# Alternating two token tiles between two PSUM banks in five column blocks of one feed-forward stage

## The chip, the cores and the metric

The program runs on one core of a Trainium2 chip. The metric is device microseconds (us) of one execution; the time before is the median of three runs. The engines that matter here are TensorE (PE in the profile), which does matrix products and transposes, ScalarE (ACT) and VectorE (DVE), which convert and combine data, and SyncE (SP), which issues the weight loads. Each engine works through its own instructions in order.

## The reference

The reference is a two-layer decoder trunk on 256 tokens of width 1024: a first layer with a gated linear recurrence, a second with dilated attention, and a SwiGLU feed-forward block before and after each mixer, so four feed-forward stages in all. Each has this form, with an inner width of 2816:

```python
def swiglu(x, w_in, w_out):
    gate, up = jnp.split(x @ w_in, 2, axis=-1)
    return (jax.nn.silu(gate) * up) @ w_out
...
x = layer_norm(DEEPNORM_ALPHA * x + 0.5 * swiglu(x, ffn_w_in[layer, 1], ffn_w_out[layer, 1]),
               ln_g[layer, 2], ln_b[layer, 2])
```

## The kernel before

All matrices are float32, and every product of two of them is made as three products of parts: each operand is split into a high part (`_hi`, rounded to the matrix unit's short form) and the rest (`_lo`), and `mm3` (line 93 and on) adds hi·hi, hi·lo and lo·hi into one PSUM bank. Line 91 is the one place that issues a product, line 101 the one that issues a transpose.

Weights arrive as half pieces of 128 x 1024 floats (512 KB). `half_piece` loads one into `raw` (six buffers), ScalarE casts it to `w_hi` (line 130; line 107 for weights that are sums), VectorE subtracts to `w_lo` (line 131; line 108), with nine buffers for each. Loads, casts and subtractions are issued ahead of their use in the order of a list (`feed`), and a scheduler then places them among the other instructions of ScalarE and VectorE.

A feed-forward stage (`ffn`) runs over 11 column blocks j = 0 to 10; a block is 256 columns of the gate and the same 256 of the up projection, side by side in one PSUM bank of 512 columns for each of the two token tiles (128 tokens, t = 0 and 1). An ordinary block does four things:

- 24 products for each tile (8 steps k over the width of 1024, three products each) into one bank (`natural`);
- the gate: `sg` = SiLU of the first 256 columns on ScalarE (line 478), `gated` = `sg` times the other 256 on VectorE (line 481);
- `rest`, put off until a later `flush`: four transposes of `gated` on TensorE (`mm<-ident,gated`) and their split into `h_hi` on ScalarE and `h_lo` on VectorE (lines 107 and 108);
- the output products of the block two before it (`prj.part(t, j - 2, w)`), 12 for each tile, which read `h_hi` and `h_lo` of that block and add into the long-lived banks `yy`.

`flush` runs inside the block, after the products of the first tile and before the gate of that tile, and again after the second. What it finds in the list is the `rest` of an earlier block.

The stage that is changed is the second, `ffn(2, ...)`, from about 308 us to about 500 us of the span. In it blocks 3 with 4 and 7 with 8 go through `two_blocks`, a seven-product scheme over two blocks. That function finishes block j + 1 before block j: it flushes the `rest` of block 4 (of block 8) itself, and leaves that of block 3 (of block 7) in the list. Ordinary blocks under the diff are therefore 2, 5, 6, 9 and 10. After block 10 there is no output part; the tail of `finish` begins with the products of block 8 and then block 9 for the first half of the columns, 6 products each.

PSUM tiles named `mm` come from a pool of four banks in the order in which they are asked for; those named `yy` have their own two pairs.

Of the kernel before, what the change touches and what calls it, by code (L numbers as in the profile page):

```python
# [16 lines left out]
NT = SEQ // P  # L17
DM = 1024
KD = DM // P
# [19 lines left out]
PAIRS = {0: (4, 8), 1: (3, 7), 3: (3, 7)}  # L39
# [10 lines left out]
def trunk_kernel(  # L50
# [33 lines left out]
    def bank():  # L84
        return psum.tile([P, 512], F32, name="mm", bufs=4)
# [4 lines left out]
    def mm(ps, lhsT, rhs, start, stop, **kw):  # L90
        tc.keep_in_program_order(nc.tensor.matmul(ps, lhsT=lhsT, rhs=rhs, start=start, stop=stop, **kw))  # L91

    def mm3(ps, a, b, first, last, **kw):

        (ahi, alo), (bhi, blo) = a, b
        mm(ps, ahi, bhi, first, False, **kw)
        mm(ps, ahi, blo, False, False, **kw)
        mm(ps, alo, bhi, False, last, **kw)

    def turn(ps, src):  # L100
        tc.keep_in_program_order(nc.tensor.transpose(ps, src, ident))  # L101
# [4 lines left out]
    def split(hi, lo, src):  # L106
        nc.scalar.copy(hi, src)  # L107
        nc.vector.tensor_tensor(lo, src, f32(hi), ALU.subtract)  # L108

    def duo(tag, bufs, pool=act, shape=(2, SEQ)):  # L110
        hi = pool.tile([P, *shape], F32R, name=f"{tag}_hi", bufs=bufs)
        lo = pool.tile([P, *shape], F32R, name=f"{tag}_lo", bufs=bufs)
        return hi, lo

    def at(pair, *idx):
        return pair[0][(slice(None),) + idx], pair[1][(slice(None),) + idx]
# [35 lines left out]
    def take(n=2):  # L152

        pump(n - len(ready))
        w, ready[:n] = ready[:n], []
        return w
# [15 lines left out]
    def cols(w, start, n):  # L172
        h, c = divmod(start, HALF)
        return at(w[h], slice(c, c + n))

    def tok(t):
        return slice(t * P, (t + 1) * P)

    def halves(ps):
        return ps.rearrange("p (m s) -> p m s", m=2)  # L180

    xT = [act.tile([P, KD, SEQ], F32R, name=f"xT{i}") for i in range(2)]
# [20 lines left out]
    def late_loads():  # L203
        for dst_, src in ((xn[0], x[tok(0), :]), (xn[1], x[tok(1), :]), (par, rg_par), (dst, dist), (qsc, q_scale)):
            tc.keep_in_program_order(nc.sync.dma_start(dst_, src))

    def softplus_prep():
        lam = par[:, 7 * KR:8 * KR]
        tmp = work.tile([P, 5, KR], F32, name="spt", tag="hh")
        t = [tmp[:, i, :] for i in range(5)]  # L210
        nc.scalar.activation(t[0], lam, AF.Abs)
        nc.scalar.activation(t[0], t[0], AF.Exp, scale=-1.0)
        nc.vector.tensor_scalar_add(t[1], t[0], 2.0)
        nc.vector.reciprocal(t[1], t[1])
        nc.vector.tensor_mul(t[1], t[0], t[1])
        nc.vector.tensor_mul(t[2], t[1], t[1])
        nc.vector.tensor_scalar_mul(t[3], t[2], 1.0 / 19.0)
        for d in (17.0, 15.0, 13.0, 11.0, 9.0, 7.0, 5.0, 3.0):
            nc.vector.scalar_tensor_tensor(t[3], t[3], 1.0 / d, t[2], ALU.add, ALU.mult)
        nc.vector.scalar_tensor_tensor(t[3], t[3], 1.0, t[1], ALU.add, ALU.mult)  # L220
        nc.vector.tensor_scalar(t[4], lam, -1.0, 0.0, ALU.mult, ALU.max)
        nc.vector.scalar_tensor_tensor(t[4], t[3], 2.0, t[4], ALU.mult, ALU.add)
        for i, f in enumerate((4.0, -8.0)):
            nc.vector.tensor_scalar_mul(sp[i], t[4], f)

    def load_ln(i, tag="o", bufs=4):
        gb = [[act.tile([P, 512], F32, name="gb", tag=f"{tag}_{('hi', 'lo')[j]}", bufs=bufs) for j in range(2)]
              for _ in range(2)]
        for r in range(2):
            for h in range(2):  # L230
                tc.keep_in_program_order(
                    nc.sync.dma_start(gb[r][h], ln[i, r, h * 512:(h + 1) * 512].partition_broadcast(P)))
        return gb
# [82 lines left out]
    def natural(ps, t, w, ks=range(KD)):  # L316

        for k in ks:
            mm3(ps, at(xT, k, tok(t)), cols(w[k // 4], (k % 4) * 512, 512), k == 0, k == KD - 1)

    def channel_half(ps, w, m):
        for k in range(KD):
            mm3(ps, cols(w, k * 256 + m * P, P), at(xT, k), k == 0, k == KD - 1)
# [75 lines left out]
        for i in range(NJ - TAIL, NJ):  # L399
            order(w_out[idx, i])  # L400

    def ffn(ln_i, turn_x, ahead, pairs=()):
        hs, gated = {}, {}
        later = []
        sums = {}
# [32 lines left out]
        def two_blocks(j):  # L438

            xs = [act_.rearrange("p k s -> p (k s)") for act_ in sums["tmp"]]  # L440
            flat = lambda n: xs[n]
            part = lambda q, t: (lambda k: at(xT, 4 * q + k, tok(t)))
            named = lambda n: (lambda k: at(sums[n], k))
            a, b, c = (bank() for _ in range(3))
            product(a, part(0, 0), True, False)
            nc.scalar.copy(flat(0), a)
            product(c, named("s1"), True, False)
            nc.scalar.copy(flat(1), c)
            flush()
            product(b, named("s2"), True, False)  # L450
            nc.vector.tensor_tensor(flat(2), b, flat(0), ALU.add)
            product(c, named("s4"), False)
            nc.vector.tensor_tensor(flat(3), c, flat(2), ALU.add)
            gate(flat(3), 0, j + 1)
            w = take()
            for t in range(NT):
                prj.part(t, j - 2, w)
            product(b, named("s3"), False, False)
            nc.vector.tensor_tensor(flat(2), b, flat(0), ALU.add)
            nc.vector.tensor_tensor(flat(1), flat(1), flat(2), ALU.add)  # L460
            gate(flat(1), 1, j + 1)
            product(a, part(1, 0), False)
            gate(a, 0, j)
            product(b, part(1, 1), False)
            nc.vector.tensor_tensor(flat(0), b, flat(0), ALU.add)
            flush()
            gate(flat(0), 1, j)
            w = take()
            for t in range(NT):
                prj.part(t, j - 1, w)  # L470

        def flush(keep=0):
            while len(later) > keep:
                later.pop(0)()

        def gate(ps, t, j):
            sg = work.tile([P, 256], F32, name="sg")
            nc.scalar.activation(sg, ps[:, :256], AF.Silu)  # L478
            if t == 0:
                gated[j] = work.tile([P, NT, 256], F32, name="gated", tag="sc")  # L480
            nc.vector.scalar_tensor_tensor(gated[j][:, t, :], ps[:, 256:], 0.5, sg, ALU.mult, ALU.mult)  # L481

            def rest():
                hh = gated.pop(j)
                pt = bank()
                for m in range(2):
                    for t_ in range(NT):
                        turn(pt[:, (m * NT + t_) * P:(m * NT + t_ + 1) * P], hh[:, t_, m * P:(m + 1) * P])
                split(*hs[j], halves(pt))
            if t:  # L490
                later.append(rest)
# [4 lines left out]
        if turn_x:  # L496
            gb = load_ln(ln_i)
            w = [take() for _ in range(3)]
            opened = []
            for t in range(NT):  # L500
                ps = bank()
# [5 lines left out]
                ps = bank()  # L507
# [9 lines left out]
        else:  # L517
            with pinned():
                ps = [[bank() for _ in range(NT)] for _ in range(2)]
                for q in range(4):  # L520
# [4 lines left out]
                    for j in range(2):  # L525
                        w = take(1)
# [10 lines left out]
        for j in range(2, NJ):  # L537
            if j == LATE and not turn_x:
                late_loads()
                gb = load_ln(ln_i)  # L540
                softplus_prep()
            if j - 1 in pairs:
                continue
            hs[j] = duo("h", HBUFS)
            if j in pairs:
                hs[j + 1] = duo("h", HBUFS)
                two_blocks(j)
                continue
            w = [take() for _ in range(2)]
            for t in range(NT):  # L550
                ps = bank()
                natural(ps, t, w)
                flush(1 - t if j == 2 else 0)
                gate(ps, t, j)
            if j == 2 and pairs:
                sum_x()
            if 0 <= j - 2 < NJ - TAIL:
                w = take()
                for t in range(NT):
                    prj.part(t, j - 2, w)  # L560
        for i in range(NJ - 2, NJ - TAIL):
            w = take()
# [394 lines left out]
    order_ffn(3)  # L957

    turn_x = ffn(0, None, 4, PAIRS.get(0, ()))
    with pinned():  # L960
        turn_x = recurrent(1, turn_x)
    turn_x = ffn(2, turn_x, 4, PAIRS.get(1, ()))
    kv = keys_values(turn_x)
    pump(6)
    turn_x = ffn(3, lambda h: None, 4)
    with pinned():
        turn_x = attention(kv, 4, turn_x)
# [77 lines left out]
```

## Time and profile before

| what | value |
|---|---|
| median of 3 runs | 1047.36 us (1046.35 to 1047.64) |
| the profiled execution | 1048.89 us, of which the span of the profile is 1047.1 us |
| TensorE busy | 1019.5 us, 97% of the span |
| VectorE busy | 774.5 us, 74% |
| ScalarE busy | 568.7 us, 54% |
| DMA | 192.70 MB, mean 184 GB/s |

The span is the time from the first to the last instruction of the program in one profiled execution. Busy shares are means over stages that differ, and a TensorE that is busy is not at its peak, since its products overlap in the records: a product of 512 columns is recorded with about 0.39 us while the next begins about 0.23 us after it.

### The profile page before, as it was taken

To read this page: it belongs to the slowest core of one execution; us is meant where nothing else is said; L and a number is where in the kernel's file an instruction comes from. 1 tells how busy PE (TensorE), PEld (TensorE's weight loads), DVE (VectorE), ACT (ScalarE), POOL (GpSimd) and SP (SyncE) were. 2 spreads that over 40 slices of the span, in tenths; PEclk is the share of its full clock that TensorE was granted. 3 is DMA by queue.
4 is the path that set the end of the run, shared out by engine and by line. 5 is a ranking of instruction groups with operands and counts; after the bars stand their busy time and mean duration, and the time that the engine had idled before them with its cause. 6 is when DMAs were issued, how large, how long until landed. Compare 5 with 4: busy or idle time off the path is not lost.

```text
span 1047.1 us, 13806 instructions
## 1 busy us (share of the span) xinstructions
PE 1019.5 (97%) x5233; PEld 853.4 (82%) x5233; DVE 774.5 (74%) x997; ACT 568.7 (54%) x790; POOL 12.0 (1%) x18
## 2 busy tenths in 40 slices
PE   8999999999899999999999999999999999999997
PEld 6787887899777888888898888888998778888885
DVE  6979877686789888777736454557677889888864
ACT  5647555359955564654435344442776755564740
POOL 0000000000000000000000000000000000000000
PEclk9999999999899999999999999999999999999999
DMA  8639458175263483672756555642533544483641
GB/s 300 243 103 339 158 195 305 62 281 173 84 228 141 138 272 140 230 286 101 263 200 203 198 186 177 200 164 99 182 122 121 181 141 151 141 281 132 240 161 41
DMA packets 55650, 192.70 MB, mean 184 GB/s; under 512 B 6432, under 2 KB 6688, under 8 KB 55584
## 3 DMA queue, kind: packets, MB, share of 16 engines
q1 hardware_dynamic: 55584, 191.83, 53.4%
q8 instruction: 41, 0.67, 0.3%
q14 instruction: 25, 0.20, 0.1%
HBM read 190.75 MB, written 1.05 MB: 183 GB/s over the span
## 4 chain that ended last, share of the span: by engine, by line
PE 83%; DVE 7%; ACT 3%; DMA 3%; issue 2%; POOL 0%; SPq 0%; DVEq 0%; ACTq 0%; POOLq 0%
PE mm L91 51%; PE yy L91 29%; PE mm L101 3%; DVE w_lo L131 2%; DMA raw<-in_w_in_dram 2%; DVE w_lo L108 1%; DMA raw<-in_w_out_dram 1%; ACT w_hi L130 1%; DVE xn L257 1%; DVE xT L108 1%; DVE xn L244 1%; DVE st L245 1%; ACT th L104 1%; ACT w_hi L107 0%; ACT L104 0%
## 5 line engine op out<-in xcount | busy, mean ns | idle before, releaser
L131 DVE TENSOR_TENSOR w_lo<-raw,w_hi 128x1024 fp32r<-128x1024 f32 (+1 forms) x295 | 352.1, 1217 | 118.0 <-ACT w_hi L130 111.2
L91 PE MATMUL mm<-w_hi,xT 128*128 128x512 f32 x1296 | 417.6, 393 | 2.6 <-DVE gated L481 1.2
L130 ACT CAST w_hi<-raw 128x1024 fp32r<-128x1024 f32 (+1 forms) x294 | 301.5, 1048 | 178.1 <-PE yy L91 70.6
L91 PEld LDWEIGHTS mm<-w_hi,xT 128*128 128x128 f32 x1296 | 242.8, 188 | 57.3 <-DVE xT L108 2.9
L91 PE MATMUL mm<-w_lo,xT 128*128 128x512 f32 x648 | 253.0, 390 | 2.2 <-DVE w_lo L131 2.2
L91 PEld LDWEIGHTS mm<-w_lo,xT 128*128 128x128 f32 x648 | 121.8, 188 | 28.0 <-DVE w_lo L131 4.0
L91 PE MATMUL yy<-w_hi,h_hi 128*128 128x512 f32 x352 | 138.9, 395 | 0.0
L91 PE MATMUL yy<-w_lo,h_hi 128*128 128x512 f32 x352 | 137.3, 390 | 0.0
L91 PE MATMUL yy<-w_hi,h_lo 128*128 128x512 f32 x352 | 137.3, 390 | 0.0
L107 ACT CAST w_hi<-raw 128x1024 fp32r<-128x1024 f32 x84 | 86.0, 1052 | 65.4 <-DVE raw L342 31.1
L108 DVE TENSOR_TENSOR w_lo<-raw,w_hi 128x1024 fp32r<-128x1024 f32 x84 | 100.6, 1219 | 14.4 <-ACT w_hi L107 14.0
L91 PE MATMUL mm<-xT,w_hi 128*128 128x256 f32 x480 | 88.6, 286 | 0.0
L91 PEld LDWEIGHTS yy<-w_lo,h_hi 128*128 128x128 f32 x352 | 66.2, 188 | 14.1 <-DVE w_lo L131 0.8
L91 PEld LDWEIGHTS yy<-w_hi,h_lo 128*128 128x128 f32 x352 | 66.1, 188 | 13.9
L91 PEld LDWEIGHTS yy<-w_hi,h_hi 128*128 128x128 f32 x352 | 66.1, 188 | 13.1
L91 PEld LDWEIGHTS mm<-xT,w_hi 128*128 128x128 f32 x480 | 74.7, 191 | 2.4 <-issue 2.0
L478 ACT ACTIVATE sg<-mm 128x256 f32<-128x256 f32 x70 | 26.6, 381 | 88.1 <-PE mm L91 87.8
L91 PE MATMUL mm<-xT,w_lo 128*128 128x256 f32 x240 | 67.9, 283 | 0.0
L481 DVE SCALAR_TENSOR_TENSOR gated<-mm,sg 128x256 f32<-128x256 f32 x70 | 29.1, 419 | 47.0 <-ACT sg L478 47.0
L91 PE MATMUL mm<-w_hi,s 128*128 128x512 f32 x192 | 62.7, 393 | 0.0
L342 DVE TENSOR_TENSOR raw<-raw 128x1024 f32<-128x1024 f32 x48 | 57.7, 1218 | 1.8 <-DMA raw<-in_w_in_dram 1.6
L91 PEld LDWEIGHTS mm<-xT,w_lo 128*128 128x128 f32 x240 | 45.9, 191 | 0.0
(132 smaller groups left out, 995.0 us busy)
## 6 DMA issues: line engine op xcount, KB each, us to landing
raw<-in_w_in_dram SPq DMA_DIRECT2D x175, 512.0 KB, 4.9
raw<-in_w_out_dram SPq DMA_DIRECT2D x88, 512.0 KB, 5.0
raw<-in_q_w_dram SPq DMA_DIRECT2D x20, 512.0 KB, 4.5
raw<-in_rg_in_dram SPq DMA_DIRECT2D x16, 512.0 KB, 4.8
gb<-in_ln_dram SPq DMA_DIRECT2D x24, 256.0 KB, 5.7
raw<-in_rg_out_dram SPq DMA_DIRECT2D x10, 512.0 KB, 3.9
raw<-in_v_w_dram SPq DMA_DIRECT2D x8, 512.0 KB, 5.1
raw<-in_k_w_dram SPq DMA_DIRECT2D x8, 512.0 KB, 5.6
```

Source lines behind the costliest of these rows:

```text
L91: tc.keep_in_program_order(nc.tensor.matmul(ps, lhsT=lhsT, rhs=rhs, start=start, stop=stop, **kw))
L101: tc.keep_in_program_order(nc.tensor.transpose(ps, src, ident))
L104: tc.keep_in_program_order(nc.scalar.activation(dst_, src, f, **kw))
L107: nc.scalar.copy(hi, src)
L108: nc.vector.tensor_tensor(lo, src, f32(hi), ALU.subtract)
L130: (nc.scalar.copy if high is nc.scalar else high.tensor_copy)(w[0][:, c], raw[:, c])
L131: i = low.tensor_tensor(out=w[1][:, c], in0=raw[:, c], in1=f32(w[0][:, c]), op=ALU.subtract)
L244: nc.vector.scalar_tensor_tensor(z, z, ALPHA, y, ALU.mult, ALU.add)
L245: nc.vector.bn_stats(self.st[:, h, :], z)
L342: nc.vector.tensor_tensor(raw[out, h], raw[x, h], raw[y, h], ALU.subtract)
L478: nc.scalar.activation(sg, ps[:, :256], AF.Silu)
L481: nc.vector.scalar_tensor_tensor(gated[j][:, t, :], ps[:, 256:], 0.5, sg, ALU.mult, ALU.mult)
```

## The change

The second feed-forward stage gets a flag, `side_by_side`. In its ordinary blocks both banks are asked for at once, and a new function, `natural_two`, issues the 48 products of the block so that the two tiles take turns: each weight part is multiplied with tile 0 into one bank and at once with tile 1 into the other. `flush` then runs once, after all 48, and both gates come after it. The other stages, and the paired blocks of this stage, stay as they are.

```diff
+    def natural_two(ps, w):
+
+        for k in range(KD):
+            bhi, blo = cols(w[k // 4], (k % 4) * 512, 512)
+            for n in range(3):
+                for t in range(NT):
+                    ahi, alo = at(xT, k, tok(t))
+                    a, b = ((ahi, bhi), (ahi, blo), (alo, bhi))[n]
+                    mm(ps[t], a, b, k == 0 and n == 0, k == KD - 1 and n == 2)
...
-    def ffn(ln_i, turn_x, ahead, pairs=()):
+    def ffn(ln_i, turn_x, ahead, pairs=(), side_by_side=False):
...
             w = [take() for _ in range(2)]
-            for t in range(NT):
-                ps = bank()
-                natural(ps, t, w)
-                flush(1 - t if j == 2 else 0)
-                gate(ps, t, j)
+            if side_by_side:
+                ps = [bank() for _ in range(NT)]
+                natural_two(ps, w)
+                flush()
+                for t in range(NT):
+                    gate(ps[t], t, j)
+            else:
+                for t in range(NT):
+                    ps = bank()
+                    natural(ps, t, w)
+                    flush(1 - t if j == 2 else 0)
+                    gate(ps, t, j)
...
-    turn_x = ffn(2, turn_x, 4, PAIRS.get(1, ()))
+    turn_x = ffn(2, turn_x, 4, PAIRS.get(1, ()), True)
```

The numbers at the names below are the program's tile numbers. In the order of TensorE at block 5, tiles `h_hi_3079` and `h_lo_3080` are the two parts of block 3, `gated_3288` is its gated product, and `mm_3385` and its neighbour are the banks of block 5. Before the change the transposes stand between the two tiles:

```order
L91 MATMUL mm_3385<-w_lo_3381,xT0_73 128x512
L91 MATMUL mm_3385<-w_hi_3380,xT1_74 128x512
L101 MATMUL mm_3410<-ident_75,gated_3288 128x128 x4
L91 MATMUL mm_3421<-w_hi_3362,xT0_73 128x512
L91 MATMUL mm_3421<-w_lo_3363,xT0_73 128x512
...
L91 MATMUL mm_3421<-w_hi_3380,xT1_74 128x512
L91 MATMUL yy_3053<-w_hi_3450,h_hi_3079 128x512
L91 MATMUL yy_3053<-w_lo_3451,h_hi_3079 128x512
L91 MATMUL yy_3053<-w_hi_3450,h_lo_3080 128x512
```

The same place after the change:

```order
L91 MATMUL mm_3385<-w_lo_3381,xT0_73 128x512
L91 MATMUL mm_3386<-w_lo_3381,xT0_73 128x512
L91 MATMUL mm_3385<-w_hi_3380,xT1_74 128x512
L91 MATMUL mm_3386<-w_hi_3380,xT1_74 128x512
L101 MATMUL mm_3435<-ident_75,gated_3288 128x128 x4
L91 MATMUL yy_3053<-w_hi_3450,h_hi_3079 128x512
L91 MATMUL yy_3053<-w_lo_3451,h_hi_3079 128x512
L91 MATMUL yy_3053<-w_hi_3450,h_lo_3080 128x512
```

The four transposes of block 3 have moved behind the second tile's products, and the output products of block 3 follow them directly. The order at block 9 is the same with block 7 in the place of block 3.

In the order of ScalarE at the end of block 5, before the change (`sg` are the two gates of block 5; `w_hi_3620` is the first weight piece of the pair 7 with 8):

```order
L130 CAST w_hi_3500<-raw_3499 128x1024
L478 ACTIVATE sg_3417<-mm_3385 128x256
L107 CAST h_hi_3079<-mm_3410 128x512
L130 CAST w_hi_3506<-raw_3505 128x1024
L130 CAST w_hi_3576<-raw_3575 128x1024
L130 CAST w_hi_3582<-raw_3581 128x1024
L478 ACTIVATE sg_3446<-mm_3421 128x256
L107 CAST w_hi_3620<-raw_3618 128x1024
```

And after it:

```order
L130 CAST w_hi_3500<-raw_3499 128x1024
L130 CAST w_hi_3506<-raw_3505 128x1024
L130 CAST w_hi_3576<-raw_3575 128x1024
L130 CAST w_hi_3582<-raw_3581 128x1024
L488 ACTIVATE sg_3442<-mm_3385 128x256
L488 ACTIVATE sg_3446<-mm_3386 128x256
L107 CAST w_hi_3620<-raw_3618 128x1024
L107 CAST h_hi_3079<-mm_3435 128x512
```

The first gate and the cast of `h_hi` have moved behind three weight casts, and `h_hi` now stands behind both gates and one more weight cast.

In the order of VectorE at the same place, before the change:

```order
L131 TENSOR_TENSOR w_lo_3501<-raw_3499,w_hi_3500 128x1024
L481 SCALAR_TENSOR_TENSOR gated_3419<-mm_3385,sg_3417 128x256
L108 TENSOR_TENSOR h_lo_3080<-mm_3410,h_hi_3079 128x512
L131 TENSOR_TENSOR w_lo_3507<-raw_3505,w_hi_3506 128x1024
L131 TENSOR_TENSOR w_lo_3577<-raw_3575,w_hi_3576 128x1024
L131 TENSOR_TENSOR w_lo_3583<-raw_3581,w_hi_3582 128x1024
L481 SCALAR_TENSOR_TENSOR gated_3419<-mm_3421,sg_3446 128x256
L108 TENSOR_TENSOR w_lo_3621<-raw_3618,w_hi_3620 128x1024
```

And after it:

```order
L131 TENSOR_TENSOR w_lo_3583<-raw_3581,w_hi_3582 128x1024
L491 SCALAR_TENSOR_TENSOR gated_3444<-mm_3385,sg_3442 128x256
L491 SCALAR_TENSOR_TENSOR gated_3444<-mm_3386,sg_3446 128x256
L108 TENSOR_TENSOR w_lo_3621<-raw_3618,w_hi_3620 128x1024
L108 TENSOR_TENSOR h_lo_3080<-mm_3435,h_hi_3079 128x512
```

`h_lo` has moved from the middle of the block to behind both gates and the subtraction of the first weight piece of the next pair. At the ends of blocks 9 and 10 `h_hi` and `h_lo` stand in the same way behind both gates and one more weight piece.

## Rows read from the trace of the kernel before

**Rows 1.** From the page: the chain that ended last, by engine.

```profile
PE 83%; DVE 7%; ACT 3%; DMA 3%; issue 2%; POOL 0%; SPq 0%; DVEq 0%; ACTq 0%; POOLq 0%
```

**Rows 2.** Busy time by engine from block 5 to 480 us; PEclk is granted clock.

```profile
core 0: us, PE busy (x) PEld busy (x) DVE busy (x) ACT busy (x) POOL busy (x), PEclk, DMA share, GB/s
381.60:480.00 98.40, 98.40 (x449) 81.41 (x448) 76.25 (x80) 54.12 (x66) 0.00 (x0) 1.00 0.65 223
```

**Rows 3.** Timeline of TensorE around block 5: start, length, instruction, count, idle before.

```profile
381.40 0.39 PE L91 MATMUL yy<-w_hi,h_lo 128*128 128x512 f32 x1
381.62 0.39 PE L91 MATMUL mm<-w_hi,xT 128*128 128x512 f32 x1
...
387.07 0.60 PE L101 MATMUL mm<-ident,gated 128*128 128x128 f32 x4
387.43 0.48 PE L91 MATMUL mm<-w_hi,xT 128*128 128x512 f32 x1
387.74 0.39 PE L91 MATMUL mm<-w_lo,xT 128*128 128x512 f32 x1
...
392.98 0.39 PE L91 MATMUL yy<-w_hi,h_hi 128*128 128x512 f32 x1
```

**Rows 4.** Timeline of ScalarE at block 5.

```profile
390.10 0.37 ACT L478 ACTIVATE sg<-mm 128x256 f32<-128x256 f32 x1
390.38 0.58 ACT L107 CAST h_hi<-mm 128x512 fp32r<-128x512 f32 x1
...
394.57 1.06 ACT L130 CAST w_hi<-raw 128x1024 fp32r<-128x1024 f32 x1 [1.67 <-DMA raw<-in_w_out_dram]
395.53 0.37 ACT L478 ACTIVATE sg<-mm 128x256 f32<-128x256 f32 x1
395.83 1.05 ACT L107 CAST w_hi<-raw 128x1024 fp32r<-128x1024 f32 x1
```

**Rows 5.** Timeline of VectorE at the end of block 5.

```profile
395.66 1.23 DVE L131 TENSOR_TENSOR w_lo<-raw,w_hi 128x1024 fp32r<-128x1024 f32 x1 [1.00 <-ACT w_hi L130]
396.80 0.42 DVE L481 SCALAR_TENSOR_TENSOR gated<-mm,sg 128x256 f32<-128x256 f32 x1
397.13 1.22 DVE L108 TENSOR_TENSOR w_lo<-raw,w_hi 128x1024 fp32r<-128x1024 f32 x1
```

**Rows 6.** Timelines at block 9: TensorE's first product, then ScalarE and VectorE.

```profile
446.12 0.39 PE L91 MATMUL mm<-w_hi,xT 128*128 128x512 f32 x1
...
456.58 1.05 ACT L130 CAST w_hi<-raw 128x1024 fp32r<-128x1024 f32 x1 [0.17 <-DVE w_lo L131]
...
458.62 1.05 ACT L130 CAST w_hi<-raw 128x1024 fp32r<-128x1024 f32 x1 [0.50 <-DMA raw<-in_w_out_dram]
...
458.81 0.42 DVE L481 SCALAR_TENSOR_TENSOR gated<-mm,sg 128x256 f32<-128x256 f32 x1
459.70 1.23 DVE L131 TENSOR_TENSOR w_lo<-raw,w_hi 128x1024 fp32r<-128x1024 f32 x1 [0.47 <-ACT w_hi L130]
```

**Rows 7.** Timelines at block 10, all engines.

```profile
462.92 0.39 PE L91 MATMUL mm<-w_hi,xT 128*128 128x512 f32 x1
...
468.36 0.60 PE L101 MATMUL mm<-ident,gated 128*128 128x128 f32 x4
...
469.62 0.69 DVE L108 TENSOR_TENSOR h_lo<-mm,h_hi 128x512 fp32r<-128x512 f32 x1 [0.21 <-ACT h_hi L107]
...
474.29 0.39 PE L91 MATMUL yy<-w_hi,h_hi 128*128 128x512 f32 x1
...
474.77 1.04 ACT L130 CAST w_hi<-raw 128x1024 fp32r<-128x1024 f32 x1
...
475.85 1.23 DVE L131 TENSOR_TENSOR w_lo<-raw,w_hi 128x1024 fp32r<-128x1024 f32 x1
```

**Rows 8.** TensorE's longest waits before, and the stretch after the longest.

```profile
159.69 0.55 PE L101 MATMUL mm<-ident,gated 128*128 128x128 f32 x3 [2.12 <-DVE gated L481]
...
276.09 0.80 PE L91 MATMUL yy<-w_hi,kv 128*128 128x512 f32 x1 [4.66 <-ACT kv L107]
...
276.10:281.60 5.50, 5.50 (x13) 4.22 (x14) 5.19 (x10) 5.29 (x7) 0.00 (x0) 0.50 0.30 98
159.70:165.00 5.30, 5.30 (x25) 4.45 (x26) 5.30 (x8) 4.40 (x6) 0.00 (x0) 1.00 0.73 255
```

## The prediction, written before the result was known

> **What bounds the kernel now.** I read the chain of waits first: 83% of the span is TensorE [rows 1], so in most stretches the time is the sum of TensorE's own work, and an instant in which it waits is lost. Then the stretch that changes: from 381.6 to 480 us TensorE is busy 98.40 of 98.40 us, at a granted clock of 1.00 (the level of 2.4 GHz), while VectorE has 76.25 and ScalarE 54.12 us of work [rows 2]. There is no wait in these blocks for the change to take away. Last, the timelines of the three engines at each block's end, since the change touches the order there.
>
> **What the change leaves as it is.** It adds and removes no product: five blocks (2, 5, 6, 9 and 10) keep 48 products each, 240 in all. A block's 24 products of one tile take 387.07 - 381.62 = 5.45 us, 0.227 us each [rows 3]. Whether the alternation changes this pace has no row that alternates at every product. The nearest are those where the bank changes between neighbours: from the last `yy` product to the first `mm` product of block 5 it is 381.62 - 381.40 = 0.22 us, the same pace [rows 3]. So I take 0. The bounds: a product has 512 columns, which at 2.4 GHz are 0.213 us, so at most 0.014 us x 240 = 3.4 us could be gained; for a loss nothing speaks, and I keep 1 us. The four transposes take 0.36 us until the next product, and that one holds the next for 0.31 instead of 0.23 us [rows 3]; they are moved, not multiplied, so 0.
>
> The second bank is taken with a block's second product instead of 24 products later. It has to be read out by then. In block 6 it is the bank of block 5's first tile; that tile's gate now runs after the block (0.37 us on ScalarE, 0.42 on VectorE [rows 4, 5]) and is covered by the 24 output products between the blocks, 5.45 us. Cost 0; without that cover it would be these 0.8 us. Loads keep their order on SyncE, and no weight is wanted earlier: in the first 24 products only the first half of a block's weights is read.
>
> The Trainium skill's page Perfetto Trace Analysis, section Matmuls, advises that independent groups rotate through banks, so that ScalarE and VectorE empty one while the next group's products run. Before, that is so: block 5's first gate starts at 390.10, under the second tile's products (387.43 to 392.98) [rows 3, 4]. By that rule alone the change would expose two gates for each block, at most 5 x 2 x 0.8 = 8 us, if the next products needed those banks; by the rows they don't, so I charge nothing for it.
>
> **What the change moves on to the path.** Before, the transposes of the put-off block stand between the tiles, and 24 products (5.45 us) hide the split into `h_hi` and `h_lo`. Now they stand after both tiles. Where the next products read that very block, nothing hides it. This is so at block 5 (output of block 3, which the paired scheme leaves for last), at block 9 (output of block 7), and, 6 products later, after block 10 (output of block 9). At block 6 the output is that of block 4, split long before, and at block 2 the flush stood behind both tiles already: 0 each.
>
> *Block 5.* The 48 products run from 381.62 for 48 x 0.227 = 10.90 us, to 392.52. Transposes 0.36, next product 0.31, next 0.23: the third output product, the first that reads `h_lo`, could start at 393.42 [rows 3]. ScalarE comes to the first gate only after the cast that waits for a load until 394.57 (the load's issue precedes the change's reach, so it stays); gates at 395.53 and, 0.30 later as the rows are spaced, 395.83; the cast of the next weight piece at 396.13, 1.05 long; `h_hi` 0.58 more, done at 397.76 [rows 4]. VectorE: `w_lo` at 395.66, gates at 396.80 and 397.13, the next `w_lo` at 397.46 for 1.22, to 398.68 [rows 5], then `h_lo` 0.69 [rows 7]: 399.37. Wait: 399.37 - 393.42 = 5.95 us. Most of it is queue: casts and subtractions for weights that are wanted a block later stand ahead of the split. Behind the waiting products stands all of TensorE.
>
> *Block 9.* Start 446.12 [rows 6], third output product 446.12 + 10.90 + 0.36 + 0.31 + 0.23 = 457.92. The gates fit between the casts at 456.58 and 458.62; the latter waits for a load, then VectorE's `w_lo` runs from 459.70 to 460.93 [rows 6] and `h_lo` to 461.62. Wait: 3.70 us. I take rows as they stand, since the weights' distance to TensorE is set by buffers again before this block.
>
> *Block 10.* Start 462.92 [rows 7]; `h_lo` of block 9 is read by the ninth product of the tail: 462.92 + 10.90 + 0.36 + 0.31 + 7 x 0.227 = 476.08. The products end 0.44 us earlier than before (no transposes among them: 0.36 + 0.08), and with them the last gate, the cast at 474.77 and the `w_lo` at 475.85, so 475.41 + 1.23 + 0.69 = 477.33 [rows 7]. Wait: 1.25 us.
>
> *Restart.* After each wait the first product holds the next for 0.08 us more, as after the transposes [rows 3]: 3 x 0.08 = 0.24.
>
> Sum: 5.95 + 3.70 + 1.25 + 0.24 = 11.1 us. Nothing gives it back: TensorE has no wait for weights later in the stage [rows 2], and the following stages need its output. Against the profiled execution's own 1048.89 us (span 1047.1 and 1.8 around it) that is 1060.0; this execution was 1.5 above the median of 1047.36, so I predict 1047.36 + 11.1 = 1058.5 us.
>
> **Bounds of the waits.** From below: the split alone, with both engines free, ends `h_lo` at 469.62 + 0.69 = 470.31, 1.95 us after its transposes begin at 468.36 [rows 7], against 0.90 us until the third output product: 1.05 us at blocks 5 and 9, none in the tail (2.26 us), 2.1 us in all. In between: if the loads hold no cast up (1.67 us at block 5 [rows 4], 0.50 at block 9 [rows 6]), 11.1 - 2.2 = 8.9 us. I take the full sum, since its rows are from these very places. From above, the clock, below.
>
> **The rivals.**
> The clock falls. At block 5 TensorE would stand still from about 393.1 (the transposes' end, 392.52 + 0.60) to 397.76, 4.6 us. After an idle time of 4.66 us the granted clock was 0.50 (1.2 GHz) from 276.1 to 281.6, 13 products in 5.5 us; after one of 2.12 us it stayed 1.00 [rows 8]. Price: 5.50 - 13 x 0.227 = 2.5 us, so 1061. The idle time is next to the row that fell, but the kernel has that row once; block 9's, some 2.6 us, is nearer to the other.
>
> The queues move ahead. If casts and loads run earlier than in the rows, the waits shrink towards 2.1 to 8.9 us: 1049.5 to 1056. The prefetch loses one gate and one split inside each block, about 2 us of VectorE and ScalarE work, which speaks for a little of it; the in-order loads speak against much.
>
> The other side: the bank is what holds the pace. If a product had to wait for the one before it in its own bank, alternation would give up to 3.4 us. It decides for faster only if the three waits sum to less than that, close to their lower bound of 2.1: 1047.36 - 3.4 + 2.1 = 1046.1. With my 11.1 it would leave 1055.1. Against it stands the unchanged pace at a change of bank [rows 3].
>
> That the change does nothing: the transposes move, but both splits are served at once and no bank matters, 1049.7; within reach of no change only if a little of the 2.1 us is hidden.
>
> **How the numbers follow.** A difference of 0.2% (2.1 us) is about what a measurement of this kernel can tell from none. Three waits at full clock, 1056 to 1060: 0.60. The clock falls as well, 1060 to 1063: 0.20. Queues ahead or a bank gain beside the waits, 1050 to 1056: 0.13. Hardly any wait: 0.04. Gain from the banks and short waits: 0.03. The range from 1054.5 to 1062.5 holds the first case, most of the second and a part of the third, about 8 in 10. All of the first three are slower: 0.94; same 0.04, faster 0.02.
>
> **What would show it.** In the changed kernel's trace TensorE waits before the first and third `yy` product after blocks 5 and 9 and before `h_lo` of block 9 in the tail, released by `h_hi` and `h_lo`, some 6, 3.7 and 1.2 us; the 48 products of a block still take 10.9 us; no wait at blocks 2 and 6; the stages after keep their lengths. I am wrong if the 48 products take less, if the waits are near 1 us, or if the clock falls after block 5.

## The result, and the profile after

The changed kernel takes 1061.59 us (median of 4 runs, 1061.08 to 1062.95) beside 1047.3 us of the kernel before in the same session: a ratio of 1.014, with a 95% interval of 1.0122 to 1.0157. That is slower by 14.3 us; the forecast was 1058.5, within 1054.5 to 1062.5. The profiled execution took 1062.95 us with a span of 1061.2, so the spans differ by 14.1 us. One execution of one kernel below (flush after a quarter) took 1449.89 us, far outside all others, and is left out of that kernel's interval.

On the page, the chain that ended last and the first row of busy times (the chain before is in [rows 1]):

```profile
PE 76%; DVE 11%; DMA 5%; ACT 4%; issue 2%; POOL 0%; SPq 0%; DVEq 0%; ACTq 0%; POOLq 0%
...
PE 1026.8 (97%) x5233; PEld 857.5 (81%) x5233; DVE 775.0 (73%) x997; ACT 568.3 (54%) x790; POOL 11.9 (1%) x18
```

TensorE's share of the chain fell from 83% to 76%, and what it lost went to VectorE, DMA and ScalarE: TensorE now waits for them in places. Its busy time rose by 7.3 us with no product added, which waits alone can't do. The windows show where most of it is (columns as in [rows 2]): first the 48 products of blocks 5 and 6, then the stretches after blocks 5 and 9.

```profile
core 0: us, PE busy (x) PEld busy (x) DVE busy (x) ACT busy (x) POOL busy (x), PEclk, DMA share, GB/s
381.90:392.90 11.00, 11.00 (x51) 9.04 (x50) 9.40 (x9) 7.24 (x7) 0.00 (x0) 1.00 0.88 316
404.80:415.70 10.90, 10.90 (x49) 8.98 (x49) 10.24 (x9) 4.73 (x5) 0.00 (x0) 1.00 0.15 48
...
398.10:401.60 3.50, 3.49 (x8) 2.81 (x9) 2.23 (x2) 0.00 (x0) 0.00 (x0) 0.51 0.40 143
466.40:473.20 6.80, 5.82 (x13) 4.13 (x14) 2.15 (x4) 0.47 (x1) 0.00 (x0) 0.50 0.81 327
```

A block of alternating products still takes 10.9 us without a gap. After blocks 5 and 9 the granted clock is 0.5, the lower of its levels (1.2 GHz), for 3.4 and 6.8 us. TensorE's timeline after blocks 5, 9 and 10, in that order ([rows 3, 6, 7] are before's):

```profile
392.89 0.60 PE L101 MATMUL mm<-ident,gated 128*128 128x128 f32 x4
396.74 0.50 PE L91 MATMUL yy<-w_hi,h_hi 128*128 128x512 f32 x1 [3.26 <-ACT h_hi L107]
397.08 0.39 PE L91 MATMUL yy<-w_lo,h_hi 128*128 128x512 f32 x1
398.11 0.80 PE L91 MATMUL yy<-w_hi,h_lo 128*128 128x512 f32 x1 [0.64 <-DVE h_lo L108]
398.71 0.63 PE L91 MATMUL yy<-w_hi,h_hi 128*128 128x512 f32 x1
399.13 0.63 PE L91 MATMUL yy<-w_lo,h_hi 128*128 128x512 f32 x1
...
404.85 0.39 PE L91 MATMUL mm<-w_hi,xT 128*128 128x512 f32 x1
...
463.54 0.60 PE L101 MATMUL mm<-ident,gated 128*128 128x128 f32 x4
466.93 0.80 PE L91 MATMUL yy<-w_hi,h_hi 128*128 128x512 f32 x1 [2.79 <-ACT h_hi L107]
...
468.61 0.79 PE L91 MATMUL yy<-w_hi,h_lo 128*128 128x512 f32 x1 [0.46 <-DVE h_lo L108]
...
475.88 0.39 PE L91 MATMUL mm<-w_hi,xT 128*128 128x512 f32 x1
...
486.76 0.60 PE L101 MATMUL mm<-ident,gated 128*128 128x128 f32 x4
...
490.24 0.50 PE L91 MATMUL yy<-w_hi,h_lo 128*128 128x512 f32 x1 [0.64 <-DVE h_lo L108]
```

How to read it: four transposes and 24 output products take 0.36 + 0.31 + 23 x 0.227 = 5.89 us when nothing waits (the pace of [rows 3]). After block 5 they take 404.85 - 392.89 = 11.96, so 6.1 us are lost there; after block 9 475.88 - 463.54 = 12.34, so 6.45. The wait can be told apart from the clock. The third output product should follow the transposes after 0.90 us. It comes at 398.11 and 468.61, late by 4.32 and 4.17 us; the rest, some 1.7 and 2.2, is one restart of 0.08 each and products that stand 0.43 us apart (398.71 and the next, 399.13) where they stood 0.227. In the tail the ninth product, due at 486.76 + 0.36 + 0.31 + 7 x 0.227 = 489.02, comes at 490.24: 1.22 us late. The whole tail loses 1.35. The sum is 6.1 + 6.45 + 1.35 = 13.9 us. The stage is longer by 14.0, measured from the last four transposes of its opening (318.97 us after, 318.70 before) to the first transpose of its closing norm (502.63 and 488.37): 183.7 us after, 169.7 before. From there to the end TensorE's instructions stay 14.1 to 14.3 us behind those of before; nothing is given back.

The waits' cause stands in the timelines of ScalarE and VectorE at block 5 ([rows 4, 5] are before's):

```profile
393.15 1.04 ACT L130 CAST w_hi<-raw 128x1024 fp32r<-128x1024 f32 x1 [0.23 <-PE mm L91]
394.10 0.65 ACT L488 ACTIVATE sg<-mm 128x256 f32<-128x256 f32 x2
395.16 1.04 ACT L107 CAST w_hi<-raw 128x1024 fp32r<-128x1024 f32 x1 [0.41 <-DMA raw<-in_w_in_dram]
396.11 0.58 ACT L107 CAST h_hi<-mm 128x512 fp32r<-128x512 f32 x1
...
395.37 0.75 DVE L491 SCALAR_TENSOR_TENSOR gated<-mm,sg 128x256 f32<-128x256 f32 x2
396.24 1.23 DVE L108 TENSOR_TENSOR w_lo<-raw,w_hi 128x1024 fp32r<-128x1024 f32 x1
397.38 0.68 DVE L108 TENSOR_TENSOR h_lo<-mm,h_hi 128x512 fp32r<-128x512 f32 x1
```

`h_hi` needs the transposes of 392.89, and 0.58 us of ScalarE. It gets its turn at 396.11, behind a weight cast, two gates and another weight cast. `h_lo` stands behind both gates and the subtraction of that second weight piece.

### The profile page after: what moved, and what is told of

The parts are those of the page before. It is cut to its first block, busy times and chain, and to the rows that moved or that the text cites. A ratio compares the mean times of both kernels' runs of the same rounds, so it can differ in the third digit from the quotient of the medians.

```text
span 1061.2 us, 13806 instructions
## 1 busy us (share of the span) xinstructions
PE 1026.8 (97%) x5233; PEld 857.5 (81%) x5233; DVE 775.0 (73%) x997; ACT 568.3 (54%) x790; POOL 11.9 (1%) x18
## 3 DMA queue, kind: packets, MB, share of 16 engines
HBM read 190.75 MB, written 1.05 MB: 181 GB/s over the span
## 4 chain that ended last, share of the span: by engine, by line
PE 76%; DVE 11%; DMA 5%; ACT 4%; issue 2%; POOL 0%; SPq 0%; DVEq 0%; ACTq 0%; POOLq 0%
PE mm L91 47%; PE yy L91 27%; DVE w_lo L131 4%; DMA raw<-in_w_in_dram 4%; PE mm L101 3%; DMA raw<-in_w_out_dram 2%; DVE w_lo L108 2%; ACT w_hi L130 1%; ACT w_hi L107 1%; DVE xn L257 1%; DVE xT L108 1%; DVE xn L244 1%; DVE raw L352 1%; DVE st L245 1%; ACT th L104 0%
## 5 line engine op out<-in xcount | busy, mean ns | idle before, releaser
L91 PE MATMUL mm<-w_hi,xT 128*128 128x512 f32 x1296 | 409.5, 393 | 1.9 <-DVE gated L491 1.2
L91 PE MATMUL mm<-w_lo,xT 128*128 128x512 f32 x648 | 246.5, 390 | 1.5 <-DVE w_lo L131 1.5
L91 PE MATMUL yy<-w_hi,h_hi 128*128 128x512 f32 x352 | 141.9, 403 | 6.2 <-ACT h_hi L107 6.0
L91 PE MATMUL yy<-w_hi,h_lo 128*128 128x512 f32 x352 | 139.9, 398 | 1.7 <-DVE h_lo L108 1.7
L91 PE MATMUL yy<-w_lo,h_hi 128*128 128x512 f32 x352 | 139.6, 396 | 0.1
```

## The experiments

Theory A is that of the prediction: the place of `flush` costs the time, through waits for a split that stands late in two queues, and the alternation is free. Its main rival, B, is that the alternation itself (or both gates coming late) costs. A third question is what share the clock has. The kernels ran in two sessions, in which the kernel before took 1046.76 us (19 runs; late flush, flush in the middle, blocks 2 and 6, the filled wait) and 1045.88 us (23 runs; the others). A trace is of one execution of each kernel. All but the last kernel have the code of before ahead of the changed stage, yet their traces reach its opening transposes between 315.5 and 319.0 us; so the lengths of the stage are compared, and not whole traces.

**Late flush without alternation.** Products tile after tile as before; `flush` and the gates where the change puts them in the source. (The scheduler moves the first gate back ahead of three weight casts: at block 5 ScalarE does it at 390.25 us.)

```diff
-                natural_two(ps, w)
+                for t in range(NT):
+                    natural(ps[t], t, w)
```

> The tiles run one after the other as before, but both banks are taken at once and the transposes stand after the second tile, as in the change; the scheduler puts the first gate back between the weight casts, so one gate less stands ahead of the split. Theory: nearly the whole loss, waits of about 3.9, 3.5 and 1 us after blocks 5, 9 and 10 and the clock falling in one or both, 1057 to 1061 us. Rival (the alternation is at fault): 1047 to 1049 us.

Measured: 1060.42 us (4 runs), ratio 1.0139 (1.012 to 1.0159), beside 1.014 of the whole change. The stage is 11.3 us longer than before. TensorE after block 5:

```profile
392.54 0.60 PE L101 MATMUL mm<-ident,gated 128*128 128x128 f32 x4
397.00 0.50 PE L91 MATMUL yy<-w_hi,h_hi 128*128 128x512 f32 x1 [3.87 <-ACT h_hi L107]
...
398.38 0.79 PE L91 MATMUL yy<-w_hi,h_lo 128*128 128x512 f32 x1 [0.64 <-DVE h_lo L108]
```

The same waits, with the products in the old order. The third output product is late by 398.38 - 392.54 - 0.90 = 4.94 us here, and the clock falls. After block 9 TensorE stood still for 1.52 and 0.64 us, the third output product was 2.6 us late and the clock did not fall there, so this kernel lost 2.7 us at a place where the changed one lost 6.45. The medians of the two kernels lie 13.7 and 14.3 us above those of before; of the stage, the traced execution shows 11.3 us beside 14.0.

**Alternation with the flush in the middle.** The 48 products alternate, but `flush` runs after 24 of them. (Block 2 keeps its flush at the end, as before the change.)

```diff
-    def natural_two(ps, w):
+    def natural_two(ps, w, half=None):
...
         for k in range(KD):
+            if half and k == KD // 2:
+                half()
...
-                natural_two(ps, w)
+                natural_two(ps, w, flush if j > 2 else None)
```

> The two tiles alternate as in the change, but the four transposes of the earlier block stand after 24 of the 48 products in blocks 5, 6, 9 and 10, where they stood before. Theory (the loss is the transposes' new place): the waits after blocks 5, 9 and 10 are gone, the clock stays up, 1047 to 1048 us. Rival (products that alternate between banks are slower, or two gates at a block's end cost): the 48 products take longer than 10.9 us or waits stay, 1050 us or more.

Measured: 1048.62 us (10 runs), ratio 1.002 (1.0007 to 1.0033); the stage is 0.8 us longer, at a granted clock of 1.00 from 320 to 488 us. The median lies between the two forecasts. One wait is left in the changed blocks, after block 9:

```profile
456.24 0.39 PE L91 MATMUL yy<-w_lo,h_hi 128*128 128x512 f32 x1
456.95 0.50 PE L91 MATMUL yy<-w_hi,h_lo 128*128 128x512 f32 x1 [0.32 <-DVE h_lo L108]
```

Moving `flush` back by 24 products takes away 13.2 of the 14.0 us that the stage had lost. `h_lo` still stands late in VectorE's queue after block 9: 0.71 us between these two products in place of 0.23.

**Flush after a quarter.** As the last, but after 12 of the 48 products. (The last is the "first experiment" of the expectation.)

```diff
+            if half and k == KD // 4:
+                half()
```

> As the first experiment, but with the transposes after 12 of the 48 products, so that 36 products hide the split. Theory (the first experiment's rest was its one wait of 0.6 us after block 9, where 24 products did not hide the split): that wait is gone and the time is that of before, 1046 to 1048 us. Rival (alternating products have a small cost of their own): 1048 to 1050 us with no wait to show for it.

Measured: 1048.04 us (12 runs; 1047.94 without the one at 1449.89), ratio 1.0013 (1.0004 to 1.0022), on the border between the two forecasts. No wait is left in the changed blocks, and the stage is 170.2 us long, 0.5 more than before; 0.4 of that arise in the paired blocks 3 and 4, whose products are those of before. A stage of the same code as before's, in the kernel with the flag on the third stage (below), was 0.3 shorter than before's. So with the split early the alternation costs and gives nothing that blocks 5, 6, 9 and 10 show. The ratio stands for 1.4 us; where the rest of it lies I could not find in the trace, and a cost of that size is not excluded.

**Only blocks 2 and 6.** The two blocks whose output products read a block that was split long before.

```diff
-            if side_by_side:
+            if side_by_side and j in (2, 6):
```

> The change in blocks 2 and 6 alone, where the next output products read a block that was split long before. Theory: no wait, 1047 to 1048 us. Rival (each alternating block costs something of its own): two fifths of the loss of 14.3 us, about 1053 us.

Measured: 1047.17 us (10 runs), ratio 1.0004 (0.9992 to 1.0016); stage 0.2 us longer, no wait at either block. Alternation, late flush and late gates cost nothing where the following products don't read what was flushed.

**The change in the third stage instead.** There no blocks are paired: nine ordinary blocks, 432 alternating products, and each block's output products read one that was flushed a block earlier.

```diff
-    turn_x = ffn(2, turn_x, 4, PAIRS.get(1, ()), True)
+    turn_x = ffn(2, turn_x, 4, PAIRS.get(1, ()))
...
-    turn_x = ffn(3, lambda h: None, 4)
+    turn_x = ffn(3, lambda h: None, 4, (), True)
```

> The change in the third feed-forward stage in place of the second. That stage has no paired blocks, so each ordinary block's output products read a block that was split long before, and only the tail reads one just transposed. Theory: one wait of 1.3 us in the tail and nothing else, 1048 to 1049 us, although nine blocks alternate in place of five. Rival (a cost of each alternating block): 1060 us or more.

Measured: 1048.04 us (11 runs), ratio 1.0021 (1.0012 to 1.003). The third stage took 222.1 us, 1.3 more than before's 220.8. The only waits in it are in its tail, where block 9's split is read at once:

```profile
705.20 0.40 PE L91 MATMUL yy<-w_hi,h_lo 128*128 128x512 f32 x1
705.70 0.49 PE L91 MATMUL yy<-w_hi,h_hi 128*128 128x512 f32 x1
706.03 0.40 PE L91 MATMUL yy<-w_lo,h_hi 128*128 128x512 f32 x1
707.08 0.50 PE L91 MATMUL yy<-w_hi,h_lo 128*128 128x512 f32 x1 [0.65 <-DVE h_lo L108]
```

The products at 705.70 and 707.08 come 0.28 and 0.81 us late; with two restarts the tail loses 1.35 us, as in the changed kernel. Nine blocks with both gates late lose nothing beside it.

**The split ahead of both gates.** The whole change, but the order on ScalarE and VectorE is forced: the gates stand behind `h_hi` and `h_lo`, and so does each weight piece that comes nine or more pieces later (the number of weight buffers; nearer ones can't be put behind it, since TensorE needs them first).

```diff
+            if side_by_side and ahead_of:
+                tc.add_manual_dep(act_i.ins, ahead_of[0].ins.name, NO_SYNC, reason="behind the split")
...
+        for n, a, v in behind:
+            if made[0] >= n:
+                tc.add_manual_dep(hi.ins, a.ins.name, NO_SYNC, reason="behind the split")
+                tc.add_manual_dep(lo.ins, v.ins.name, NO_SYNC, reason="behind the split")
```

> The change, with one thing altered: on ScalarE and VectorE the split of the earlier block stands ahead of both gates and of the weight piece that is wanted last, so that only the pieces that stood there anyway are before it. Theory (most of each wait is the queue ahead of the split, and the clock falls only because the waits are long): waits of some 2.2 us after blocks 5 and 9, none in the tail, clock at 1.00 in both, 1051 to 1053 us. Rival (the split's own length makes the wait): 1059 us or more.

Measured: 1054.8 us (4 runs), ratio 1.0082 (1.0065 to 1.01); stage 5.5 us longer. TensorE after block 5, and one of the waits that are new:

```profile
378.66 0.50 PE L91 MATMUL yy<-w_lo,h_hi 128*128 128x512 f32 x1 [0.75 <-DVE w_lo L139]
...
395.52 0.50 PE L91 MATMUL yy<-w_hi,h_hi 128*128 128x512 f32 x1 [0.67 <-ACT h_hi L107]
395.86 0.40 PE L91 MATMUL yy<-w_lo,h_hi 128*128 128x512 f32 x1
396.25 0.50 PE L91 MATMUL yy<-w_hi,h_lo 128*128 128x512 f32 x1
```

The third output product is late by 396.25 - 394.25 - 0.90 = 1.10 us after block 5 (its transposes begin at 394.25) and 1.16 after block 9, none in the tail, and the clock stays at 1.00. With the restarts these places lose 1.24 and 1.30 us in place of 6.1 and 6.45. So the split itself is one us of each wait, and the rest is the queue ahead of it. The time is longer than the theory had it, for the forced order has a price elsewhere: TensorE is late in the paired blocks, some 3.0 us in all, where its two longest waits are for `w_lo` (0.75 in the row above). The median is 8.9 us above before's, the traced stage 5.5; what the executions that were not traced lost more is not shown. Both forecasts missed the time.

**The wait filled with products.** The whole change, and 14 products after block 5 and 12 after block 9, behind `flush`, into a bank that nothing reads. They add work and change no output.

```diff
+FILL = {5: 14, 9: 12}
...
                 flush()
+                if j in FILL:
+                    spare = bank()
+                    x0 = xT[0].rearrange("p k s -> p (k s)")
+                    for n in range(FILL[j]):
+                        mm(spare, x0[:, :P], x0[:, :512], n == 0, n == FILL[j] - 1)
```

> The change, with products that nobody reads put behind the transposes of blocks 5 and 9 (14 and 12, 0.227 us each, so 3.2 and 2.7 us), which is less than TensorE waits there, so they delay nothing; they take one bank more from the pool. Theory (idle TensorE let the granted clock fall to 0.50 after both blocks, worth about 4 us): the clock stays at 1.00 and the time is 1057 to 1058.5 us. Rival (the fall has another cause, or the rest of the loss is not the clock): 1061 to 1062 us.

Measured: 1056.21 us (4 runs), ratio 1.0097 (1.0075 to 1.0119); stage 9.0 us longer. TensorE after block 5 (the added line moves the numbers of the lines below it by one; x10 are those of the 14 added products that lie in the stretch asked for), then the window around it:

```profile
390.80 2.45 PE L92 MATMUL mm<-xT 128*128 128x512 f32 x10
393.37 0.50 PE L92 MATMUL yy<-w_hi,h_hi 128*128 128x512 f32 x1
393.71 0.40 PE L92 MATMUL yy<-w_lo,h_hi 128*128 128x512 f32 x1
395.06 0.50 PE L92 MATMUL yy<-w_hi,h_lo 128*128 128x512 f32 x1 [0.95 <-DVE h_lo L109]
```

```profile
core 0: us, PE busy (x) PEld busy (x) DVE busy (x) ACT busy (x) POOL busy (x), PEclk, DMA share, GB/s
385.00:400.00 15.00, 13.92 (x63) 10.88 (x62) 11.46 (x12) 7.14 (x10) 0.00 (x0) 1.00 0.73 279
```

TensorE still can't go on before `h_lo`, but with work in the gap the clock stays at 1.00 in the whole stage. The stage is 14.0 - 9.0 = 5.0 us shorter than that of the changed kernel, with 26 products more. Of that at most some 3.9 us answer to the clock (worked out below), and some 1.1 us do not: the split after block 9 was ready before the 2.7 us of added products ended, where it came 4.17 us late in the changed kernel, so that wait was itself shorter. The price of the clock is bounded by this run, not measured alone.

**Alternation with the flush in the middle, in all four stages.** The second experiment's `natural_two`, with the flag on every stage.

```diff
-    turn_x = ffn(0, None, 4, PAIRS.get(0, ()))
+    turn_x = ffn(0, None, 4, PAIRS.get(0, ()), True)
...
-    turn_x = ffn(3, lambda h: None, 4)
+    turn_x = ffn(3, lambda h: None, 4, (), True)
...
-    ffn(5, turn_x, 0, PAIRS.get(3, ()))
+    ffn(5, turn_x, 0, PAIRS.get(3, ()), True)
```

> Alternating tiles with the transposes after 24 of 48 products in the ordinary blocks of all four feed-forward stages. A block's later weights are then wanted up to 24 products later, which could help the first stage, whose waits are for weights. Theory: those waits lie in the paired blocks and stay, so 1046 to 1049 us. Rival (weights come too late in ordinary blocks): 1043 us or less.

Measured: 1053.99 us (6 runs), ratio 1.0074 (1.0062 to 1.0087). Most of the loss is one place in the first stage, after block 2:

```profile
41.87 1.03 PE L101 MATMUL mm<-ident,gated 128*128 128x128 f32 x8
46.12 0.50 PE L91 MATMUL yy<-w_hi,h_hi 128*128 128x512 f32 x1 [3.21 <-ACT h_hi L107]
46.45 0.40 PE L91 MATMUL yy<-w_lo,h_hi 128*128 128x512 f32 x1
47.49 0.79 PE L91 MATMUL yy<-w_hi,h_lo 128*128 128x512 f32 x1 [0.65 <-DVE h_lo L108]
48.09 0.63 PE L91 MATMUL yy<-w_hi,h_hi 128*128 128x512 f32 x1
```

The first stage makes its blocks 0 and 1 together, so both are still in the list at block 2 (eight transposes in the first row, where the other stages have four). Before, `flush(1)` turned block 0 between the two tiles; now it is turned at the end of the block, its split is read at once, and the clock falls: 5.9 us lost. That is the mechanism of block 5 at a place that I had not looked at; both theories had it wrong.

## Why the prediction was right, and where its sizes were off

**The alternation is free: right as far as the traces show.** The 48 products of block 5 take 10.9 us, as predicted. With an early split (flush after a quarter) the four alternating blocks behind the first pair add some 0.1 us, and 432 products in the third stage cost nothing beside the tail. Theory B falls with these and with the late flush alone, whose ratio is 1.0139 beside 1.014 of the whole change. The gain of up to 3.4 us, the bound that I had left for the banks, does not exist here. The medians leave room for a cost of some 1 us (ratios 1.002 and 1.0013 with the flush moved back) that no trace places.

The Trainium skill's page Perfetto Trace Analysis, section Matmuls, would have independent groups rotate through banks so that one is emptied under the next one's products; by that rule alone the gates, no longer under a tile's products, would have cost up to 8 us. The third stage shows 0 for nine blocks. In its blocks TensorE waited only where the next products need what is made from the bank, as in the tail.

**Waits after blocks 5, 9 and 10: right in place and cause, 9.7 us in place of 10.9.** Block 5: 4.32 us, predicted 5.95. The mis-sized part is the load. The last weight cast ahead of the gates was taken to start at 394.57, after 1.67 us of waiting for a load [rows 4]; that is 12.95 us after the block's first product. Here it started at 393.15, 11.15 us after that product (382.00). The change is not what did it: in the kernel with the flag on the third stage, whose second stage has the code of before, that product and that cast start 11.29 us apart:

```profile
378.59 0.39 PE L91 MATMUL mm<-w_hi,xT 128*128 128x512 f32 x1
...
389.88 1.05 ACT L130 CAST w_hi<-raw 128x1024 fp32r<-128x1024 f32 x1 [0.17 <-DMA raw<-in_w_out_dram]
```

So most of those 1.67 us belonged to the one execution from which the rows were read, and the middle bound, in which no load holds a cast up (5.95 - 1.67 = 4.28), was the better term. That the change moves the queues ahead is not shown: SyncE issued the two loads of that kind from 385.39 (385.73 before), which is 0.34 us. Block 9: 4.17, predicted 3.70, of which 0.28 is the slow clock between the first two products. Tail: 1.22, predicted 1.25. The lower bound was met too: 1.05 us was worked out for the split with both engines free, and with the split forced ahead of the gates it was 1.10 and 1.16, with none in the tail.

**The clock: the step that failed.** The forecast was for full clock, with the fall as a rival at 0.20 and at block 5 only, since block 9's idle time was nearer to the 2.12 us that had left the clock alone [rows 8]. It fell at both: 3.26 us of idle time at block 5, 2.79 at block 9. The rival's price of 2.5 us came from a fall of 5.5 us; here the price is 6.1 - 4.32 - 0.08 = 1.7 us at block 5 and 6.45 - 4.17 - 0.08 = 2.2 at block 9, 3.9 us together. With waits and restarts of 9.7 + 0.24 that is 13.8 us of the stage's 14.0, where 11.1 had been predicted. A fall after block 5 was one of the prediction's own signs of being wrong, and 1061.59 us lies in the case to which it gave 0.20. That two errors had opposite signs, -1.2 in the waits and +3.9 in the clock, was luck: with the waits as forecast and the clock as measured the sum is 1058.5 + 3.9 = 1062.4, at the very edge of the range.

**No cost at blocks 2 and 6, nothing given back: right.** No wait stands there, alone or in the whole change, and the loss stays to the end (14.1 us of it in the spans).

No version that I ran beats the kernel before. There was no wait in these blocks for an alternation to remove [rows 2].

## What to carry to other kernels

When a loop is rewritten so that two tiles take turns, what costs is not the turns but the work that stood between the tiles: ask for each piece of it who reads its result, and how many products are now between. Then read the queues of the engines that make it, instruction by instruction: a split of 1 us cost 4, because casts for weights of the next block and two gates stood ahead of it in order. Where such a wait is over some 2 us, count TensorE's clock into its price as a case of its own; here it added 40% to the waits.

## What the runs showed that I had not expected

The same idle time does not always have the same effect on the clock. In the first stage every kernel has a wait ahead of three transposes between 157 and 163 us. TensorE's timeline there, the transposes and two of the products behind them, of the changed kernel and then of the one with the flush in the middle:

```profile
158.16 0.55 PE L101 MATMUL mm<-ident,gated 128*128 128x128 f32 x3 [2.29 <-DVE gated L491]
...
159.26 0.63 PE L91 MATMUL yy<-w_hi,h_hi 128*128 128x512 f32 x1
159.69 0.63 PE L91 MATMUL yy<-w_lo,h_hi 128*128 128x512 f32 x1
```

```profile
158.05 0.55 PE L101 MATMUL mm<-ident,gated 128*128 128x128 f32 x3 [2.22 <-DVE gated L493]
...
159.12 0.40 PE L91 MATMUL yy<-w_hi,h_hi 128*128 128x512 f32 x1
159.35 0.39 PE L91 MATMUL yy<-w_lo,h_hi 128*128 128x512 f32 x1
```

After 2.29 us the products stand 0.43 us apart for some 3.4 us; after 2.22 us they keep 0.23. With 2.18 and 2.23 us in two other kernels (late flush without alternation, split first) the clock fell, with 2.21 (flush after a quarter) it did not. Every idle time of 2.79 us or more that I read was followed by a fall, none of 1.9 or less. The falls lasted some 3.4 or some 6.8 us, and the one after the idle time of 4.66 us [rows 8], which all kernels have, was of either length: 3.4 us in the filled-wait and all-stages kernels, 6.8 in the other eight. The Trainium skill's page TensorE: Matmul & The Clock Gate, Part 1, says of the slow products at a kernel's start that their count differs from run to run of one kernel. The traces here show something like it for falls in the middle of kernels; what decides it in a given execution no run here shows.
